# Late adaLN columns kept behind the low part of the weight unit ahead of them, in a two-layer decoder trunk on one core

## The chip, the cores and the metric

The kernel runs on one core of one Trainium2 chip. The metric is device time in microseconds of one launch, from the inputs in the chip's main memory to the output there; less is better. A core has TensorE for matmuls (PE in the profile, PEld for its weight loads), VectorE (DVE), ScalarE (ACT), GpSimd (POOL), SyncE (SP), which here only issues loads, and 16 DMA engines that all queues share.

## What is computed

The reference is a two-layer trunk with sequence 256 and width 1024 in f32. Cut to what matters here, one layer is:

```python
mod = c_act @ ada_w + ada_b                    # c_act = silu(c), one row; ada_w is 1024 x 3072
shift, scale, gate = jnp.split(mod, 3, axis=-1)
h = rmsnorm(x, norm_g) * (1.0 + scale[:, None]) + shift[:, None]
z = h @ w_in                                   # 1024 x 13312, feeds three branches and their gates
... # branch A: conv and linear recurrence; B: dilated attention; C: gated linear attention
merged = mg[:, :, 0] * (ya @ proj_a) + mg[:, :, 1] * (yb @ proj_b) + mg[:, :, 2] * (yc @ proj_c)
return x + gate[:, None] * (merged @ w_o)
```

`mod` is a matrix times one vector. Per layer it has 24 parts of 128 values, which the kernel calls columns: 0 to 15 are shift and scale (needed before the layer's first matmul), 16 to 23 the gate (needed when the layer ends).

## The kernel before

All weights are read once, as a stream. `layer_units()` lists the 144 units of a layer, `stream()` (L84) puts both layers' units and the columns into one list of items. A unit is 128 x 768 to 128 x 1024 f32; a column is the 128 x 1024 block of `ada_w` that one column of `mod` needs. In a layer the units come as: q, k, v and bg (0 to 15), branch A and attention projections (16 to 67), the gate mA (68 to 75), the projection pA (76 to 83), branch C in four heads, each of one cq, one ck and four c units (84 to 107), mC (108 to 115), pC (116 to 123), mB (124 to 131), pB (132 to 135) and wo (136 to 143).

Columns 0 to 15 of layer 0 stand among the first 16 units. The others stand later, one behind each third unit from unit 68 on (`REST`, L81): in layer 0 its own columns 16 to 23 and then columns 0 to 15 of layer 1, the last behind unit 137; in layer 1 its columns 16 to 23. That makes 24 columns in layer 0's second half and 8 in layer 1's, so that layer 1 has none from unit 90 on.

`load_next()` issues the DMA of the next item into one of six buffers named `raw`, on SP's queue, in the order of the list (L205 for units, L208 for columns). `advance(i)` prepares items up to unit i. For a unit, ScalarE rounds the weights to `whi` (L232), VectorE subtracts to get the low part `wlo` (L233), each in one of four buffers, so that a matmul in full f32 becomes three: hi by hi, hi by lo, lo by hi (L799 to L801 with the weights as the moving operand, L807 to L809 with them as the stationary one). For a column, `ada_tile()` multiplies the block with the activated conditioning vector and sums over the row in one VectorE instruction (L334, with a small one behind it that reads the accumulator); for a scale column one more small multiply follows (L336). The loop in `layer()` calls `advance(i + 3)` ahead of the matmuls of unit i. After an item is prepared, `load_next()` asks for the item six places on.

Beside the units' matmuls the branches run as generators that `pump()` moves on. In the part of a layer that matters here VectorE also does: rotary and scaling of q and k (L562 to L568 with GpSimd, L575), the attention's running minimum and reciprocal (L608, L611), the recurrence (L529 to L542), branch C's products (L666 to L689), and the merging of the branches (L915, L921, L922, L949 to L952).

The order of the instructions on each engine isn't that of the code. The kernel is built with a scheduler that models the engines' times and gives each engine its instructions in the order in which the model finds them ready. On the chip each engine then works through its list in that order and waits at the head of it. `tc.issue_after(x)` is a constraint on that scheduler: what is made within it comes behind the instruction x.

Of the kernel before, what the change touches and what calls it, by code (L numbers as in the profile page):

```python
# [10 lines left out]
F32 = mybir.dt.float32  # L11
# [3 lines left out]
ALU = mybir.AluOpType  # L15
# [57 lines left out]
def unit_elems(u):  # L73
    return {"T": 2 * u[4], "F": 1024, "P": 1024}[u[0]]
# [52 lines left out]
def hybrid_trunk(ctx: ExitStack, tc: tile.TileContext, ws, ada, vec, gates, a2, qkg, c_t, x_t, pos, inv, eye,  # L127
                 mask, tri, rst, out):
    nc = tc.nc
    V, A, G, T, SY = nc.vector, nc.scalar, nc.gpsimd, nc.tensor, nc.sync  # L130
# [53 lines left out]
    cur = {}  # L184


    raw_t, w_t = {}, {}
    at_item = [0, 0]
    early = {}

    def load_next():
        n = at_item[0]
        if n >= len(items):
            return
        at_item[0] += 1
        it = items[n]
        if it in early:
            raw_t[n] = early[it]
            cur["sy", "a", it[2]] = SY.dma_start(out=early[it], in_=ada[it[1], it[2]]).ins
            return load_next()  # L200
        if it[0] == "u":
            e = unit_elems(units[it[1]][1])
            o = offs[it[1]]
            t = wts.tile([P, e], F32, name="raw", tag="raw", bufs=NRAW)
            cur["sy", it[1]] = SY.dma_start(out=t, in_=ws[o:o + e * P].rearrange("(p n) -> p n", p=P)).ins  # L205
        else:
            t = wts.tile([P, D], F32, name="raw", tag="raw", bufs=NRAW)
            SY.dma_start(out=t, in_=ada[it[1], it[2]])  # L208
        raw_t[n] = t

    def advance(i):

        while at_item[1] < len(items):
            n = at_item[1]
            it = items[n]
            if it[0] == "u" and it[1] > i:
                return
            at_item[1] += 1
            r = raw_t.pop(n)
            if it[0] == "u":  # L220
                e = unit_elems(units[it[1]][1])


                streamed = units[it[1]][1][0] == "T" and units[it[1]][1][1] != "bg"
                o = 16 * ((it[1] % 2 == 0) != streamed)
                hi = wts.tile([P, D + 16], F32R, name="whi", tag="whi")[:, o:o + e]
                lo = wts.tile([P, D + 16], F32R, name="wlo", tag="wlo")[:, o:o + e]
                with ExitStack() as st:
                    if it[1] < 4:
                        st.enter_context(tc.issue_after(cur["ra"]))  # L230
                        st.enter_context(tc.issue_after(cur["rv"]))
                    A.copy(hi, r)  # L232
                    V.tensor_tensor(lo, r, hi.bitcast(F32), ALU.subtract)  # L233
                w_t[it[1]] = (hi, lo)
            else:
                ada_tile(it[1], it[2], r)
            load_next()


# [64 lines left out]
    def vcol(l, c, n=1):  # L304
        return vec_sb[:, l, c:c + n]
# [24 lines left out]
    def ada_tile(l, c, w):  # L330
        a, b = acc[:, l, c:c + 1], vec_sb[:, l, V_ADA + c:V_ADA + c + 1]
        j, i = (c // 2, c % 2) if c < 16 else (c - 16, 2)
        m = mod[:, l, i, j:j + 1]
        V.tensor_tensor_reduce(w, w, crow2, 1.0, b, ALU.mult, ALU.add, a if i == 0 else m)  # L334
        if i == 0:
            V.tensor_tensor(m, a, vcol(l, V_NG + j), ALU.mult)  # L336
        if l == 0 and i == 1:
            h_tile(0, j, cur["rstd"], cur["h"])
# [24 lines left out]
    def h_tile(l, j, rstd, h):  # L363
        hi, lo = h
        t = tmp()
        V.scalar_tensor_tensor(t, x_sb[:, j], mod[:, l, 0, j:j + 1], rstd, ALU.mult, ALU.mult)
        sh = mod[:, l, 1, j:j + 1]
        a = A.activation(hi[:, j], t, AF.Identity, bias=sh)  # L368
        v = V.scalar_tensor_tensor(lo[:, j], t, sh, hi[:, j].bitcast(F32), ALU.add, ALU.subtract)  # L369
        cur["h_last"] = (a.ins, v.ins)  # L370
# [443 lines left out]
    def layer(l, h, first_extra):  # L814
# [6 lines left out]
        for i in range(base, base + per_layer):  # L821
            kind, nm, p, kk, n = units[i][1]
            advance(4 * (i // 4) + 3 if i < 12 else i + LEAD)
            if i in first_extra:
                first_extra[i]()
# [255 lines left out]
```

## Time and profile before

| | us |
|---|---|
| three runs | 904.12, 908.38, 950.62; median 908.38 |
| the profiled execution | 906.63 |
| its span, first to last instruction | 904.9 |
| outside the span | 1.7 |

The profile is of one execution. Durations and waits come from it; a wait for several semaphores is put down to the one that came last. TensorE's matmuls are pipelined, and each is shown for about 0.28 us though one starts every 0.11 to 0.12 us. A gap between two starts is therefore shown as idle time only for the part that is longer than the matmul shown before it. Start times are microseconds from the start of the span.

### The profile page before, as it was taken

How to read it: one execution, taken by the hardware profiler on the slowest of the kernel's cores; microseconds unless marked ns; L12 is line 12 of the kernel's file. 1: busy time of each engine (PE TensorE's matmuls, PEld its weight loads, DVE VectorE, ACT ScalarE, POOL GpSimd, SP SyncE). 2: the span in 40 equal slices, each digit the busy share in tenths (PEclk: the TensorE clock that was granted, in tenths of full speed). 3: DMA queues.
4: the chain of work that ended last, by engine and by line, in shares of the span. 5: the costliest groups of instructions: out<-in, count | busy, mean ns of one | idle time of the engine just before them, and what ended most of it. 6: DMA issues, size and time to landing. Idle time of an engine off the chain costs nothing.

```text
span 904.9 us, 16407 instructions
## 1 busy us (share of the span) xinstructions
PE 865.6 (96%) x6340; PEld 818.7 (90%) x6340; DVE 671.9 (74%) x1115; ACT 531.8 (59%) x897; POOL 179.1 (20%) x160
## 2 busy tenths in 40 slices
PE   3989999999999999999999999989999999999998
PEld 2978999999988888998989999979999988899998
DVE  6998899669667667656776788986896666656674
ACT  4376976686544554644454689666874545554451
POOL 0026365224000110100030525651430001000000
PEclk7999999999999999999999999999999999999999
DMA  8884456446756666676654644553567455455651
GB/s 334 309 290 138 146 174 193 141 134 195 248 184 197 205 212 201 212 236 205 224 168 148 191 146 144 176 194 117 184 205 239 163 189 166 148 173 187 191 167 47
DMA packets 52111, 170.16 MB, mean 188 GB/s; under 512 B 6240, under 2 KB 8160, under 8 KB 52032
## 3 DMA queue, kind: packets, MB, share of 16 engines
q1 hardware_dynamic: 51216, 167.04, 56.8%
q10 hardware_dynamic: 672, 1.87, 0.7%
q8 instruction: 50, 0.82, 0.4%
q0 software_dynamic: 144, 0.20, 0.2%
q14 instruction: 29, 0.24, 0.1%
HBM read 168.23 MB, written 1.05 MB: 187 GB/s over the span
## 4 chain that ended last, share of the span: by engine, by line
PE 51%; DVE 19%; DMA 12%; issue 8%; ACT 5%; POOL 4%; DVEq 0%; SPq 0%; ACTq 0%
DMA raw<-in_ada_dram 10%; PE mm L807 10%; PE mm L809 10%; PE mm L808 10%; DVE wlo L233 8%; PE mm L799 5%; PE mm L800 5%; PE mm L801 4%; POOL ss L570 2%; PE xps L177 1%; ACT whi L232 1%; DVE raw L334 1%; DVE rb L564 1%; DMA g_raw<-in_gates_dram 1%; DVE ra L562 1%
## 5 line engine op out<-in xcount | busy, mean ns | idle before, releaser
L233 DVE TENSOR_TENSOR wlo<-raw,whi 128x1024 fp32r<-128x1024 f32 (+2 forms) x288 | 335.3, 1171 | 84.5 <-ACT whi L232 83.1
L232 ACT CAST whi<-raw 128x1024 fp32r<-128x1024 f32 (+2 forms) x288 | 280.1, 976 | 185.2 <-PE mm L808 120.4
L807 PE MATMUL mm<-hhi,whi 128*128 128x256 f32 x768 | 217.1, 283 | 2.9 <-DVE rb L564 2.9
L809 PE MATMUL mm<-hhi,wlo 128*128 128x256 f32 x768 | 216.0, 282 | 3.5 <-DVE wlo L233 3.5
L808 PE MATMUL mm<-hlo,whi 128*128 128x256 f32 x768 | 215.4, 280 | 0.0
L799 PE MATMUL mm<-whi,hhi 128*128 128x384 f32 (+2 forms) x480 | 169.5, 358 | 7.2 <-ACT hhi L368 6.5
L800 PE MATMUL mm<-wlo,hhi 128*128 128x384 f32 (+2 forms) x480 | 171.3, 358 | 1.6 <-DVE wlo L233 1.4
L801 PE MATMUL mm<-whi,hlo 128*128 128x384 f32 (+2 forms) x480 | 167.6, 355 | 0.5 <-DVE hlo L369 0.5
L807 PEld LDWEIGHTS mm<-hhi,whi 128*128 128x128 f32 x768 | 146.0, 190 | 4.5 <-ACT tmp L857 2.9
L809 PEld LDWEIGHTS mm<-hhi,wlo 128*128 128x128 f32 x768 | 145.6, 190 | 4.7 <-DVE wlo L233 4.1
L808 PEld LDWEIGHTS mm<-hlo,whi 128*128 128x128 f32 x768 | 145.7, 190 | 0.3
L799 PEld LDWEIGHTS mm<-whi,hhi 128*128 128x128 f32 x480 | 92.9, 195 | 14.5 <-ACT hhi L368 7.5
L800 PEld LDWEIGHTS mm<-wlo,hhi 128*128 128x128 f32 x480 | 93.4, 195 | 9.1 <-DVE wlo L233 3.2
L334 DVE CUSTOM_DVE_ANT_0 raw<-raw,crow,vec_sb 128x1024 f32<-128x1024 f32 x38 | 48.7, 1283 | 70.2 <-DMA raw<-in_ada_dram 70.2
L801 PEld LDWEIGHTS mm<-whi,hlo 128*128 128x128 f32 x480 | 92.5, 194 | 6.7 <-DVE hlo L369 0.8
L807 PE MATMUL mm<-yhi,whi 128*128 128x256 f32 x320 | 89.9, 281 | 1.5 <-DVE mg L949 1.5
L808 PE MATMUL mm<-ylo,whi 128*128 128x256 f32 x320 | 89.4, 279 | 0.0
L809 PE MATMUL mm<-yhi,wlo 128*128 128x256 f32 x320 | 89.2, 279 | 0.0
L807 PEld LDWEIGHTS mm<-yhi,whi 128*128 128x128 f32 x320 | 60.4, 189 | 2.5 <-DVE mg L949 1.7
L809 PEld LDWEIGHTS mm<-yhi,wlo 128*128 128x128 f32 x320 | 60.1, 188 | 0.8 <-DVE mod L334 0.4
L808 PEld LDWEIGHTS mm<-ylo,whi 128*128 128x128 f32 x320 | 60.1, 188 | 0.0
L708 POOL TENSOR_TENSOR at_hl<-att_sb,at_hl 128x384 fp32r<-128x384 f32 x8 | 8.8, 1096 | 206.3 <-ACT at_hl L707 206.3
(236 smaller groups left out, 1409.2 us busy)
## 6 DMA issues: line engine op xcount, KB each, us to landing
raw<-in_ws_dram SPq DMA_DIRECT2D x192, 512.0 KB, 4.2
raw<-in_ws_dram SPq DMA_DIRECT2D x88, 384.0 KB, 3.1
raw<-in_ada_dram SPq DMA_DIRECT2D x38, 512.0 KB, 4.5
raw<-in_ws_dram SPq DMA_DIRECT2D x8, 400.0 KB, 4.6
g_raw<-in_gates_dram ACTq DMA_DIRECT2D x3, 512.0 KB, 4.5
x_sb<-in_x_t_dram SPq DMA_DIRECT2D x2, 512.0 KB, 6.6
ada_yhi<-in_ada_dram SPq DMA_DIRECT2D x2, 512.0 KB, 7.8
ada_ylo<-in_ada_dram SPq DMA_DIRECT2D x2, 512.0 KB, 9.0
```

What stands on the lines that cost most here:

```text
L177: seen[0] = T.transpose(*a, **k).ins
L232: A.copy(hi, r)
L233: V.tensor_tensor(lo, r, hi.bitcast(F32), ALU.subtract)
L334: V.tensor_tensor_reduce(w, w, crow2, 1.0, b, ALU.mult, ALU.add, a if i == 0 else m)
L562: V.tensor_tensor(ra.rearrange("p (g s) d -> p g s d", g=3), z4, ctab[l][:, i, t].unsqueeze(2).to_broadcast(bc), ALU.mult)
L570: G.tensor_tensor(ss, ss, mhalf[:, 0:12].rearrange("p (a b) -> p a b", a=2), ALU.pow)
L799: T.matmul(o, ah, wh, start=(k == 0), stop=False)
L800: T.matmul(o, ah, wl, start=False, stop=False)
L801: T.matmul(o, al, wh, start=False, stop=(k == KT - 1))
L807: T.matmul(ps[:, 0:S], hi[:, a:b], xh[:, k], start=(k == 0), stop=False)
L808: T.matmul(ps[:, 0:S], hi[:, a:b], xl[:, k], start=False, stop=False)
L809: T.matmul(ps[:, 0:S], lo[:, a:b], xh[:, k], start=False, stop=(k == nk - 1))
```

## The change

A dictionary entry `cur["lo"]` now keeps the instruction that makes a unit's low part. A column that isn't one of the first 16 of layer 0 is made under the constraint that it comes behind the last such instruction, which is that of the unit just ahead of it in the stream. The first 16 are left as they were. Loads, buffers, arithmetic and the number of instructions stay.

```diff
     raw_t, w_t = {}, {}
+    early_cols = {(0, c) for c in range(16)}
...
                     A.copy(hi, r)
-                    V.tensor_tensor(lo, r, hi.bitcast(F32), ALU.subtract)
+                    cur["lo"] = V.tensor_tensor(lo, r, hi.bitcast(F32), ALU.subtract).ins
                 w_t[it[1]] = (hi, lo)
+            elif it[1:] in early_cols:
+                ada_tile(it[1], it[2], r)
             else:
-                ada_tile(it[1], it[2], r)
+
+                with tc.issue_after(cur["lo"]):
+                    ada_tile(it[1], it[2], r)
             load_next()
```

The lists of VectorE, ScalarE and TensorE change from layer 0's unit 68 on, and again in layer 1's. Lines of the changed kernel are one higher from L188 on and five higher from L242 on: L334 is L339 there, L233 is L234.

The first place is VectorE at layer 0's mB, where `ylo` (L642) makes branch B's low part. The number behind a name tells buffers' uses apart and grows along the stream: `raw_4316` to `raw_4416` are units, `raw_4320`, `raw_4419` and `raw_4522` are columns 12, 13 and 14 of layer 1. Before:

```order
L642 SCALAR_TENSOR_TENSOR ylo_4894<-sgb_767,yhi_4893 128x1024
L334 ISA raw_4419,mod_155<-raw_4419,crow_134,vec_sb_83 128x1024
L334 ISA mod_155 128x1
L233 TENSOR_TENSOR wlo_4720<-raw_4316,whi_4719 128x1024
L233 TENSOR_TENSOR wlo_4756<-raw_4352,whi_4755 128x1024
L233 TENSOR_TENSOR wlo_4788<-raw_4384,whi_4787 128x1024
L334 ISA raw_4522,acc_156<-raw_4522,crow_134,vec_sb_83 128x1024
```

After, at the same place:

```order
L647 SCALAR_TENSOR_TENSOR ylo_4894<-sgb_767,yhi_4893 128x1024
L234 TENSOR_TENSOR wlo_4720<-raw_4316,whi_4719 128x1024
L339 ISA raw_4320,acc_156<-raw_4320,crow_134,vec_sb_83 128x1024
L339 ISA acc_156 128x1
L341 TENSOR_TENSOR mod_155<-acc_156,vec_sb_83 128x1
L234 TENSOR_TENSOR wlo_4756<-raw_4352,whi_4755 128x1024
L234 TENSOR_TENSOR wlo_4788<-raw_4384,whi_4787 128x1024
L234 TENSOR_TENSOR wlo_4820<-raw_4416,whi_4819 128x1024
L339 ISA raw_4419,mod_155<-raw_4419,crow_134,vec_sb_83 128x1024
```

In the stream column 13 follows unit `raw_4416`. It stood three units ahead of that unit's low part; now it stands right behind it. Column 12 does the same with `raw_4316`.

The second place is VectorE in layer 0's pB, where the last column, `raw_4624`, ends up. The merging steps L949, L950 and L952 of pB are there; `raw_4588` is unit 136, `raw_4621` unit 137. After, with the column that stood ahead of all of these rows before:

```order
L234 TENSOR_TENSOR wlo_5002<-raw_4588,whi_5001 128x1024
L954 SCALAR_TENSOR_TENSOR mg_4717<-mg_4717,mm_5007 128x256
L957 SCALAR_TENSOR_TENSOR mlo_4966<-mrg_2938,mhi_4965 128x256 x2
L954 SCALAR_TENSOR_TENSOR mg_4717<-mg_4717,mm_5024 128x256
L955 TENSOR_TENSOR mrg_2938<-mrg_2938,mg_4717 128x256
L234 TENSOR_TENSOR wlo_5042<-raw_4621,whi_5041 128x1024
L955 TENSOR_TENSOR mrg_2938<-mrg_2938,mg_4717 128x256
L339 ISA raw_4624,mod_155<-raw_4624,crow_134,vec_sb_83 128x1024
```

The column has moved from ahead of pB's merging into the middle of it.

The third place is VectorE at the start of layer 0's mA. `wlo_2531` to `wlo_2570` are units 69 to 71, `raw_1936` and `raw_2099` the first two late columns, `ro_2458` the keys that TensorE transposes next, `ylo_188` branch A's low part. Before:

```order
L233 TENSOR_TENSOR wlo_2531<-raw_1971,whi_2530 128x1024
L233 TENSOR_TENSOR wlo_2549<-raw_2013,whi_2548 128x1024
L233 TENSOR_TENSOR wlo_2570<-raw_2059,whi_2569 128x1024
L608 ISA pr_2699,st_2692<-ps_s_2690,m1_sb_120 128x512
L608 ISA st_2692 128x1
L575 TENSOR_TENSOR ro_2458<-ro_2458,ss_2459 128x768
```

After:

```order
L339 ISA raw_1936,mod_155<-raw_1936,crow_134,vec_sb_83 128x1024
L339 ISA mod_155 128x1
L234 TENSOR_TENSOR wlo_2531<-raw_1971,whi_2530 128x1024
L547 SCALAR_TENSOR_TENSOR ylo_188<-rt_2184,yhi_187 128x1024
L234 TENSOR_TENSOR wlo_2549<-raw_2013,whi_2548 128x1024
L580 TENSOR_TENSOR ro_2458<-ro_2458,ss_2459 128x768
L234 TENSOR_TENSOR wlo_2570<-raw_2059,whi_2569 128x1024
```

Other work has moved with the columns: the scaling of the keys (L575, L580 after) has come ahead of a low part and of the attention's step (L608). On TensorE the transposes of these keys stand ahead of unit 70's first matmul after; before, they stood behind its tenth. Layer 1 shows the same pattern at its mA.

## Rows read from the trace of the kernel before

**Rows 1.** The page: busy time of each engine, share of span, instructions.

```profile
PE 865.6 (96%) x6340; PEld 818.7 (90%) x6340; DVE 671.9 (74%) x1115; ACT 531.8 (59%) x897; POOL 179.1 (20%) x160
```

**Rows 2.** VectorE's waits, first 200 to 450 us, then 676 to 722 us: total, times, longest.

```profile
DVE raw L334 <- DMA raw<-in_ada_dram: 60.7, 22, 4.7
...
DVE raw L334 <- DMA raw<-in_ada_dram: 8.9, 5, 2.6
```

**Rows 3.** TensorE's waits, 200 to 480 us, then 676 to 722 us: total, times, longest.

```profile
PE mm L809 <- DVE wlo L233: 2.2, 2, 1.8
PE mm L807 <- DVE mg L949: 1.5, 1, 1.5
PE xps L177 <- ACT pr L612: 1.3, 2, 1.0
...
PE xps L721 <- DVE g_hi L687: 0.9, 1, 0.9
PE xps L702 <- DVE ke L678: 0.5, 1, 0.5
PE xps L720 <- ACT cv L686: 0.3, 1, 0.3
...
PE xps L177 <- ACT pr L612: 0.8, 1, 0.8
```

**Rows 4.** Busy time by stretch: stretch, width, PE, PEld, DVE, ACT, POOL, clock, DMA share, GB/s.

```profile
229.00:282.00 53.00, 51.45 (x446) 48.79 (x446) 35.35 (x62) 28.78 (x48) 0.00 (x0) 1.00 0.62 204
673.00:725.00 52.00, 51.20 (x447) 48.86 (x447) 35.22 (x61) 29.00 (x49) 0.00 (x0) 1.00 0.62 205
283.00:433.00 150.00, 145.98 (x1052) 134.18 (x1051) 101.90 (x177) 73.28 (x125) 9.59 (x13) 0.99 0.66 212
726.00:868.00 142.00, 142.00 (x1051) 131.71 (x1050) 86.40 (x131) 73.09 (x123) 8.26 (x12) 1.00 0.55 176
433.00:454.00 21.00, 19.37 (x163) 18.82 (x162) 16.22 (x32) 9.70 (x15) 0.00 (x0) 1.00 0.67 215
868.00:887.00 19.00, 19.00 (x165) 19.00 (x164) 14.01 (x29) 8.35 (x14) 0.00 (x0) 1.00 0.36 115
```

**Rows 5.** VectorE's timeline at layer 0's mB: start, us, what, idle before.

```profile
418.01 1.28 DVE L334 CUSTOM_DVE_ANT_0 raw<-raw,crow,vec_sb 128x1024 f32<-128x1024 f32 x1 [2.76 <-DMA raw<-in_ada_dram]
419.22 0.08 DVE L334 DVE_READ_ACCUMULATOR2_ANT mod<- 128x1 f32 x1
419.22 3.49 DVE L233 TENSOR_TENSOR wlo<-raw,whi 128x1024 fp32r<-128x1024 f32 x3
```

**Rows 6.** TensorE's timeline behind that, then the stretch around it.

```profile
418.38 0.28 PE L808 MATMUL mm<-hlo,whi 128*128 128x256 f32 x1
420.50 0.52 PE L809 MATMUL mm<-hhi,wlo 128*128 128x256 f32 x1 [1.83 <-DVE wlo L233]
...
418.00:426.00 8.00, 6.17 (x40) 5.96 (x39) 4.70 (x5) 2.54 (x4) 0.00 (x0) 0.79 0.67 206
```

**Rows 7.** VectorE's timeline at layer 0's pB.

```profile
436.24 1.28 DVE L334 CUSTOM_DVE_ANT_0 raw<-raw,crow,vec_sb 128x1024 f32<-128x1024 f32 x1 [4.67 <-DMA raw<-in_ada_dram]
...
437.45 2.35 DVE L233 TENSOR_TENSOR wlo<-raw,whi 128x1024 fp32r<-128x1024 f32 x2
439.72 0.74 DVE L949 SCALAR_TENSOR_TENSOR mg<-mg,mm 128x256 f32<-128x256 f32 x2
```

**Rows 8.** The page, DMA issues: what, queue, count, KB each, median us to landing.

```profile
raw<-in_ws_dram SPq DMA_DIRECT2D x192, 512.0 KB, 4.2
raw<-in_ada_dram SPq DMA_DIRECT2D x38, 512.0 KB, 4.5
```

**Rows 9.** VectorE, GpSimd and TensorE timelines at layer 0's mA.

```profile
225.46 0.95 DVE L575 TENSOR_TENSOR ro<-ro,ss 128x768 f32<-128x768 f32 x1
...
221.65 3.13 POOL L570 TENSOR_TENSOR ss<-ss,mhalf 128x12 f32<-128x12 f32 x1
...
227.22 0.82 PE L177 MATMUL xps<-eye_sb,ro 128*128 128x128 f32 x6
```

## The prediction

> **What bounds the kernel now.** The page's busy times come first: TensorE is busy 865.6 of 904.9 us, VectorE 671.9 [rows 1]. So TensorE's own work sets most of the time, and only what makes it stand still, or lowers its clock, can be won here. Second, VectorE's waits in the two stretches that hold the late columns [rows 2]: it stood 60.7 us in 22 waits and 8.9 us in 5 for columns' loads, 69.6 us in all. That isn't yet time lost. Third, therefore, TensorE's own waits in the same stretches [rows 3]: 2.2 us for low parts, 1.5 for pB's merging, 1.3 and 0.8 for the attention's probabilities, 0.9, 0.5 and 0.3 in branch C, 7.5 in all. Of ten microseconds that VectorE waits, about one reaches TensorE.
>
> The fourth view gives the size better, because the kernel has a copy of itself without late columns: layer 1 from unit 90 on. Rows 4 pair the stretches. From branch C to the end of mB layer 0 takes 150.0 us (283 to 433) and layer 1 takes 142.0 (726 to 868), with 1052 and 1051 matmuls; the layer with columns shows 4.0 us of TensorE idle, the other none. At pB and the start of wo it is 21.0 (163 matmuls) against 19.0 (165). At mA and pA both layers have columns, and idle is 53.00 - 51.45 = 1.55 and 52.00 - 51.20 = 0.80 us.
>
> The fifth view is one case from close by. At 418.01 a column begins after VectorE waited 2.76 us for its load; then three low parts follow without a pause [rows 5]. 2.76 + 1.28 + 0.08 + 3.49 is 7.6 us in which their turn was late. TensorE needs a low part and stands until 420.50, 1.83 us; and the granted clock of 418 to 426 is 0.79, that is, after standing the engine ran for a time at the lower of its two levels, 1.2 instead of 2.4 GHz [rows 6]. The 8 us gave (1 - 0.79) x 8 = 1.7 us less work than the full clock, on top of the 1.83.
>
> **Why the order did that.** VectorE works through its list in order. Before, a column stood three units ahead of its place in the stream, so its load was the youngest one wanted; a load takes 4.5 us from issue to landing [rows 8]. A unit's 24 matmuls at about 0.115 us are 2.8 us. A low part is made three units early, 8.3 us, of which cast and subtraction take about 2.3; a delay of up to about 6 us is hidden. Most waits (60.7 / 22 = 2.8 us, and 1.36 for the column itself) fit in that, which is why only a few reach TensorE.
>
> **The change part by part.** It adds and removes no instruction and no load. It moves 32 columns of 1.28 + 0.08 us on VectorE [rows 5], and with them the scheduler moves other work on VectorE, ScalarE and TensorE. SP's queue keeps its order. A column now comes six items after its load was asked for, and at least four units lie between, 4 x 2.8 = 11 us against 4.5 to land. So I take the 69.6 us of waiting as gone. Nothing is late next in its place on VectorE: in the long stretch it was busy 101.9 of 150 us [rows 4]. What TensorE gets back:
>
> 1. Branch C to mB of layer 0. At most 150.0 - 142.0 = 8.0 us: 4.0 idle, 1.7 clock, and 2.3 of gaps too short to show, since a matmul is drawn longer than its turn. At least 0, if other work is late instead. I take 7.0, near the top, because layer 1's stretch is the same program and the only thing it lacks is the columns; 1.0 is left for the columns' own time, which stays.
> 2. pB and wo of layer 0. At most 21.0 - 19.0 = 2.0. Before, the last column waited 4.67 us, and pB's first merging step came only at 439.72 [rows 7], for which TensorE stood 1.5 us [rows 3]. Now the column stands in the middle of pB's merging, with 1.36 us. If all of that is on the path and nothing else is won, the end is 1.4 us later. Between -1.4 and 2.0 I take 1.0: the 1.5 us go, and part of the column comes back.
> 3. mA and pA of both layers. At most their idle, 1.55 + 0.80 = 2.35; at least below nothing, because here the order of other work changes too (third place of the change, and the second rival). I take 1.0.
>
> The sum is 7.0 + 1.0 + 1.0 = 9.0 us. The profiled execution took 906.63, so 897.6 is forecast. That execution is 1.75 below the median of the runs shown (908.38) and 2.5 above their lowest.
>
> The Trainium skill has a page, "Perfetto Trace Analysis", whose section "Identifying Performance Opportunities" says that improving a kernel means, in general, improving its most-contended engine. By that rule a new order on VectorE would bring nothing here, and the sum would be 0. The trace doesn't bear that out in full: 8.0 us lie between two stretches with the same matmuls. But the first rival below is that case. The same page says under "Optimization Strategy" that a gap which repeats can mean too few buffers. By that, the six load buffers would be at fault, no order of VectorE would help, and the third rival would hold; 11 us of lead against 4.5 us of landing speak against it.
>
> **The rivals.** First, the waits are hidden anyway, and TensorE's gaps only move. For it: TensorE is 96% busy, nine tenths of VectorE's waiting never reached it, and the new order of TensorE's list comes from a model that may again put small transposes too early, as it did where 1.3 and 0.8 us were lost for probabilities. Against it: layer 1's stretch, which a list of the same origin serves with no idle time. With the gaps of [rows 3] replaced by as many new ones and the clock's 1.7 us won, it gives 904.9; with two thirds replaced, 906.6 - 1.7 - 2.5 = 902.4. I call 902 to 907 this case.
>
> Second, slower: the keys' transposes at mA. Before, VectorE scaled the keys at 225.46, GpSimd's factor was there at 221.65 + 3.13 = 224.8, and TensorE took the transposes at 227.22 [rows 9]. After, TensorE comes to them ten matmuls earlier, 227.22 - 1.15 = 226.1, while on VectorE a column (1.36) and branch A's low part (1.2) have come ahead of the scaling and one attention step (0.8) has gone behind it. With one column less earlier on, it would end at about 226, with no slack. If it comes d late, TensorE stands for d, and where it stands long the lower clock costs another 1.7, as in [rows 6]. The pattern is in both layers: 2 x (d + 1.7). It eats the 9.0 us from d = 2.8 on; with d = 4 it is 906.6 - 9.0 + 11.4 = 909.0. For it speaks that GpSimd's part varies and nothing waits behind it before; against it, that at most two VectorE instructions can be that late.
>
> Third, the change doesn't do what it says: columns still wait for their loads behind the low parts, because a buffer comes free later. The loads are then what the path hangs on, and the gaps stay, about 906. Against it stands the lead of 11 us.
>
> **How the numbers follow.** The forecast, 893.5 to 902 with 897.6 as its middle, gets 0.66; the first rival 0.20; the slower one 0.07; the third 0.04; more than the bounds allow (12.35 us, 894.3, less an execution's luck) 0.03. The range reaches from 893.5 over most of the first rival and the third to 906.0, and leaves out about 0.15. A measurement of this kernel can tell about 2% from no change, that is 18 us. The bounds of the terms stop at 12.35 us, so faster by over 2% gets only 0.03; slower by over 2% would need several times the second rival, 0.01; within 2% the rest, 0.96.
>
> **What would show each step right or wrong.** In the changed kernel's list of VectorE's waits the row of columns waiting for their loads should fall from 69.6 us to under 8. Layer 0's stretch from branch C to mB should have almost no TensorE idle and last 142 to 144 us, at a granted clock of 1.00; pB to wo should last 19 to 21. TensorE's waits for low parts, L721 and L702 should be gone there. The keys' transposes at mA should show no wait over 1 us in either layer. The prediction is wrong if the stretch stays over 147 us, if columns still wait for loads, or if TensorE's new list shows waits over 1.5 us with a lowered clock behind them.

## The result and the profile after

| | before | after |
|---|---|---|
| median of four runs each, us | 906.69 | 892.39 (891.68 to 894.17) |
| ratio after to before | | 0.9848, 95% interval 0.9824 to 0.9873 |
| the profiled execution, us | 906.63 | 892.15 |
| its span, us | 904.9 | 890.3 |

The change takes 1.5% off, 14.3 us by the medians and 14.5 by the profiled executions. It is less than the 2% that a measurement was taken to tell from no change, but the interval is clear of 1. One of the four runs before took 950.62 us, a slow one that the ratio leaves out; the median of the other three is 905.01, and against that the difference is 12.6 us. The forecast was 897.6, the range ended at 893.5, and the median lies 1.1 us below that.

The page of the changed kernel, busy times, the line that answers to [rows 1]:

```profile
PE 860.3 (97%) x6340; PEld 816.5 (92%) x6340; DVE 677.8 (76%) x1115; ACT 533.0 (60%) x897; POOL 176.7 (20%) x160
```

VectorE is busy 5.9 us longer than before, and the kernel is 14 us shorter. Nothing became cheaper. What went is waiting. The page's chain of waits, shares by engine, first of the kernel before:

```profile
PE 51%; DVE 19%; DMA 12%; issue 8%; ACT 5%; POOL 4%; DVEq 0%; SPq 0%; ACTq 0%
```

and of the changed kernel:

```profile
PE 71%; DVE 13%; issue 5%; POOL 4%; ACT 4%; DMA 1%; SPq 0%; DVEq 0%; ACTq 0%
```

12% of the span hung on transfers, now 1%. The page's costliest groups, the columns of the changed kernel (busy time, mean ns of one, idle time ahead of them):

```profile
L339 DVE CUSTOM_DVE_ANT_0 raw<-raw,crow,vec_sb 128x1024 f32<-128x1024 f32 x38 | 50.3, 1325 | 0.0
```

The last number is 0.0: VectorE waits for no column's load any more, where it stood 69.6 us in the two stretches of [rows 2]. TensorE's waits from 200 to 480 us, the view of [rows 3], have two lines left, both of the layer's end and as long in the kernel before (1.0 and 0.9 us), and from 640 to 720 us there is none:

```profile
PE mm L159 <- DVE rs_m L356: 1.0, 1, 1.0
PE xps L945 <- ACT tmp L379: 0.9, 1, 0.9
```

The stretches of [rows 4] in the changed kernel. The cuts lie at the same distance from the first matmul of a stage (mA, branch C, pB, wo) as there, so that nearly the same matmuls are in each: mA and pA of layer 0, of layer 1, branch C to mB of layer 0, pB and the start of wo of layer 0.

```profile
228.43:279.32 50.89, 50.89 (x446) 48.66 (x445) 36.57 (x64) 29.82 (x49) 0.00 (x0) 1.00 0.65 227
659.32:710.26 50.94, 50.94 (x447) 48.70 (x446) 36.63 (x64) 29.84 (x49) 0.00 (x0) 1.00 0.67 225
280.32:422.08 141.76, 141.76 (x1052) 131.64 (x1051) 106.76 (x177) 73.95 (x125) 9.64 (x13) 1.00 0.70 227
422.08:441.36 19.28, 19.28 (x167) 19.28 (x166) 16.01 (x34) 9.72 (x15) 0.00 (x0) 1.00 0.66 211
```

Against [rows 4] these are 2.11 us (53.00 - 50.89), 1.06 (52.00 - 50.94), 8.24 (150.00 - 141.76) and 1.72 (21.00 - 19.28) shorter, with 446, 447, 1052 and 167 matmuls where there were 446, 447, 1052 and 163. The last pair isn't like for like: by matmuls, from pB's third to the 163rd behind it, it is 433.10 to 454.39 before and 422.18 to 441.25 after, 21.29 against 19.07 and so 2.2 us shorter. In all four TensorE is busy over the whole width. Layer 0 with its columns now takes what layer 1 took without them (142.0, 19.0). With 2.2 for the last the four add up to 13.6 us; 1.0 more of the 14.6 us in the span lies outside of them.

What a column's place means is read at column 13, the one of [rows 5]. SyncE's queue and VectorE in the changed kernel, the issue of its load and its turn:

```profile
402.28 0.33 SPq L209 DMA_DIRECT2D raw<-in_ada_dram  x1
```

```profile
413.37 1.28 DVE L339 CUSTOM_DVE_ANT_0 raw<-raw,crow,vec_sb 128x1024 f32<-128x1024 f32 x1
```

That is a lead of 11.1 us. In the kernel before, the same load was issued here,

```profile
412.22 0.33 SPq L208 DMA_DIRECT2D raw<-in_ada_dram  x1
```

and VectorE came to it at 418.01 - 2.76 = 415.25 [rows 5]: a lead of 3.0 us, for a load that took 5.8 to land.

### The profile page after: what moved, and what is told of

Its sections match the earlier page's. It is cut to its first block, busy times and chain, and to the rows that moved or that the text cites. A ratio compares the mean times of both kernels' runs of the same rounds, so it can differ in the third digit from the quotient of the medians.

```text
span 890.3 us, 16392 instructions
## 1 busy us (share of the span) xinstructions
PE 860.3 (97%) x6340; PEld 816.5 (92%) x6340; DVE 677.8 (76%) x1115; ACT 533.0 (60%) x897; POOL 176.7 (20%) x160
## 4 chain that ended last, share of the span: by engine, by line
PE 71%; DVE 13%; issue 5%; POOL 4%; ACT 4%; DMA 1%; SPq 0%; DVEq 0%; ACTq 0%
PE mm L812 14%; PE mm L814 14%; PE mm L813 14%; PE mm L806 6%; PE mm L805 6%; PE mm L804 6%; DVE wlo L234 4%; POOL ss L575 2%; PE xps L177 2%; PE xps L173 2%; PE ps_s L173 1%; DVE rb L569 1%; DVE ra L567 1%; POOL ro L573 1%; ACT whi L233 1%
## 5 line engine op out<-in xcount | busy, mean ns | idle before, releaser
L234 DVE TENSOR_TENSOR wlo<-raw,whi 128x1024 fp32r<-128x1024 f32 (+2 forms) x288 | 336.5, 1172 | 109.4 <-ACT whi L233 107.6
L233 ACT CAST whi<-raw 128x1024 fp32r<-128x1024 f32 (+2 forms) x288 | 280.3, 977 | 206.8 <-PE mm L813 126.3
L339 DVE CUSTOM_DVE_ANT_0 raw<-raw,crow,vec_sb 128x1024 f32<-128x1024 f32 x38 | 50.3, 1325 | 0.0
```

Source lines behind the costliest of these rows:

```text
L234: cur["lo"] = V.tensor_tensor(lo, r, hi.bitcast(F32), ALU.subtract).ins
```

## The experiments

Each was timed beside the kernel before on the same chip, whose medians in the four sessions were 906.5 to 908.9 us. Stretches are those of the last table, cut in the same way.

| run | what | median us (range) | ratio to before, 95% interval |
|---|---|---|---|
| c1_after_again | the changed kernel again | 892.52 (892.29 to 894.74) | 0.9849 [0.9824, 0.9873] |
| e1_no_cols | columns' arithmetic left out | 893.28 (891.47 to 893.86) | 0.9838 [0.9795, 0.9882] |
| e3_first_layer | order in layer 0's half only | 894.16 (893.69 to 895.57) | 0.9854 [0.9811, 0.9897] |
| e4_second_layer | order in layer 1's half only | 905.20 (902.65 to 906.49) | 0.9964 [0.9943, 0.9984] |
| e5_one_free | column 13 set free | 892.61 (891.63 to 893.66) | 0.9831 [0.9780, 0.9883] |
| e8_back1 | one unit earlier | 891.66 (890.54 to 892.26) | 0.9823 [0.9787, 0.9859] |
| e8_back2 | two units earlier | 893.02 (892.68 to 894.22) | 0.9842 [0.9812, 0.9872] |
| e8_back3 | three units earlier | 893.42 (892.64 to 895.65) | 0.9848 [0.9816, 0.9880] |
| e8_back4 | four units earlier | 902.33 (899.29 to 906.91) | 0.9942 [0.9921, 0.9962] |
| e7_five_buffers | five load buffers | 893.76 (892.42 to 895.00) | 0.9846 [0.9822, 0.9869] |
| e10_five_back3 | five buffers, three units earlier | 910.43 (907.77 to 913.57) | 1.0026 [1.0009, 1.0044] |
| e9_triple | columns three times | 900.37 (898.40 to 900.77) | 0.9916 [0.9885, 0.9947] |
| e11_one_wait | one wait, at mB | 892.24 (891.54 to 894.87) | 0.9839 [0.9816, 0.9863] |
| e12_wait_pB | one wait, ahead of pB | 894.47 (893.73 to 895.09) | 0.9864 [0.9842, 0.9886] |
| e13_wait_pA | one wait, at pA | 892.59 (892.09 to 893.56) | 0.9845 [0.9819, 0.9871] |

### Do the columns' own 1.3 us cost anything?

```diff
                 with tc.issue_after(cur["lo"]):
-                    ada_tile(it[1], it[2], r)
+                    V.tensor_copy(mod[:, it[1], i, j:j + 1], r[:, 0:1])
```

> The changed kernel with the 32 late columns' reduction on VectorE (1.3 us each) replaced by a copy of one element of the loaded block, at the same place; the columns' products are left out, their loads stay. Theory (the gain came from taking away VectorE's waits for the columns' loads; the columns' own 1.3 us lie beside TensorE's work): 891.4 to 893.4 us, within 1 us of the changed kernel's 892.4, and the stretches of TensorE (branch C to mB of layer 0, pB, wo) as long as in the changed kernel to 0.5 us. Rival (VectorE's amount of work still bounds the stages with columns): the 24 late columns of layer 0 and the 8 of layer 1 are worth 32 x 1.3 = 42 us of VectorE, and if a tenth of it lay on the path the time is 888 us or less.

It was 893.28, no faster than with the columns. Its stretches from branch C to mB and at pB:

```profile
281.23:423.28 142.05, 142.05 (x1052) 131.75 (x1051) 89.13 (x155) 73.81 (x125) 9.75 (x13) 1.00 0.69 227
423.28:442.56 19.28, 19.28 (x167) 19.28 (x166) 14.10 (x31) 9.70 (x16) 0.00 (x0) 1.00 0.64 210
```

VectorE is busy 89.13 us there in place of 106.76, and TensorE takes 142.05 in place of 141.76. At mA and pA alone it is 0.5 us less a layer (50.35 and 50.40), which the whole time doesn't show. So from branch C to pB a column in its place is free, in the middle of pB's merging too.

### Which half of the stream gives the gain?

```diff
-            elif it[1:] in early_cols:
+            elif it[1:] in early_cols or n > 200:
```

> The changed kernel with the order kept only for the 24 late columns that stand in layer 0's half of the stream; the 8 of layer 1 stand free, as before. Theory (each stage pays for the waits of its own columns): layer 0's terms stay (mA and pA 2.1, branch C to mB 8.2, pB and wo 2.1, start 0.5), layer 1's 1.2 at pA and 0.4 ahead of it come back: 893.5 to 894.5 us. Rival (the gain is one thing, the half-speed stretch of the clock after 420 us and where the later ones fall): 891.5 to 893 us, as the changed kernel.

`n` is the item's number in the stream. It was 894.16, as the theory had it. Layer 0's stretches are the changed kernel's to 0.01 us, and the stretch of mA and pA in layer 1 is back at 52.44. The other half has `n < 200` there:

> The other half: the order kept only for the 8 late columns of layer 1; the 24 of layer 0 stand free. Theory: layer 0's stages as in the kernel before, pA of layer 1 at 29.2 us in place of 30.4: 904.5 to 906 us, 1.2 to 2 us under the kernel before, and with the kernel of layer 0's half the two gains add up to 14.3 within 1 us. Rival (the two halves are worth little apart, since the columns of one half push the other's loads about): the two gains add up to 12 us or less.

905.20; the stretch in layer 1 is 50.95, as in the changed kernel. But the two gains, 908.93 - 894.16 = 14.8 and 908.93 - 905.20 = 3.7, add up to 18.5, where the theory had 14.3 within 1 and the rival 12 or less. The whole gain on this chip is known only from a neighbour of the changed kernel, the run with column 13 set free: 908.93 - 892.61 = 16.3. And the interval of this run leaves anything from 1.5 to 5.2 us for the smaller gain. So the excess of about 2 us isn't clear of the noise. One source of that noise stands in layer 0 of this run, whose instructions come in the very order of the kernel before on VectorE, ScalarE and TensorE. Its stretches there, in an execution of 902.65 us, the fastest of ten:

```profile
228.81:280.96 52.15, 51.72 (x446) 49.20 (x446) 35.33 (x63) 28.78 (x48) 0.00 (x0) 1.00 0.67 208
...
281.96:428.97 147.01, 143.73 (x1052) 132.50 (x1051) 101.76 (x177) 73.45 (x125) 9.34 (x13) 1.00 0.69 215
428.97:452.33 23.36, 21.04 (x167) 20.84 (x166) 16.31 (x33) 9.87 (x16) 0.00 (x0) 0.93 0.62 201
```

The same order gave 53.00, 150.00 and 21.00 in [rows 4]: 1 to 3 us more or less in a stage, between two executions. The stretches of the changed kernel, which has no such waits, came out the same to the hundredth in its second profile (50.89, 50.94, 141.76 and 19.28). So an execution of the kernel before is one draw among several, its stretches too; 13 of them on that chip lay between 903.98 and 911.79.

### Place or lead: how far ahead may a column stand?

A list `los` of all units' low parts lets a column be held behind an earlier one:

```diff
-                with tc.issue_after(cur["lo"]):
+                with tc.issue_after(los[-2]):
```

(`los[-3]`, `los[-4]` and `los[-5]` for two, three and four units.)

> The changed kernel with each late column held behind the low part of one unit earlier in the stream. Theory (what a column loses is its load's lead: behind its own unit it has four to five units, 11 to 14 us, against 4.5 us to land; one unit less leaves 8 to 11 us): no waits for columns' loads, 892 to 893.5 us. Rival (what counts is that the column stands ahead of the low part that is due next, whether or not it waits): a third of the gain goes back, 896 to 898 us.

> The same with two units earlier. Theory: the lead is 5.5 to 8 us, so a few columns wait, 10 us of waits or less in all, and 892.5 to 897 us. Rival: two thirds of the gain go back, 901 to 903 us.

> The same with three units earlier, which is about where the columns stood in the kernel before. Theory: the lead is 2.8 to 5.5 us, most columns wait, 40 to 70 us in all, and the time is 900 to 908 us with a stand of TensorE of over 1 us in mB or pB of layer 0. Rival (the gain came from the other work that moved on the engines when the columns were put under a constraint at all): below 897 us.

With one and two units there is no wait for a column's load and the time is 891.66 and 893.02. With three it is still 893.42, far from the 900 to 908 that the theory gave. VectorE's waits for columns there, in total, times and longest:

```profile
DVE raw L341 <- DMA raw<-in_ada_dram: 5.0, 7, 1.3
```

The theory had the place of the columns before wrong by one: most of them stood ahead of four low parts that come before them in the stream, not three (in VectorE's list of the kernel before, 4 for most, 3 to 5 for the rest). So four was run.

> Each late column held behind the low part of four units earlier, so that four low parts that come before it in the stream are still to be made when it is worked on, as in the kernel before; with three to be made it was 893.4 us. Theory (the step is sharp, because with six buffers a column's load can't be asked for until the item six places ahead is done, and with four low parts still to come that item is the one just ahead of it on VectorE; with three there is one unit's time between): waits for columns' loads of 50 to 70 us in all, and 900 to 907 us. Rival (the constraint moved other work too, and that gave the gain): 892 to 896 us.

902.33, and the waits are back:

```profile
DVE raw L341 <- DMA raw<-in_ada_dram: 52.2, 26, 4.4
```

One unit of difference is worth 8.9 us, and the constraint as such isn't what gave the gain. But 5.9 us (908.20 - 902.33) of the gain stay even here. In this order no column stands ahead of five low parts, where 6 of the 32 did before; what else goes into the 5.9 wasn't tested.

Why the step is so sharp: a load is issued when VectorE has set a buffer free. At column 13 with four units that is the end of a low part at 406.20 + 1.22 = 407.42. One more unit's low part and branch B's lie between it and the column's turn at 413.20 - 2.71 = 410.49. That is a lead of 3.0 us, as in the kernel before, for a load that lands after 5.8:

```profile
407.45 0.33 SPq L210 DMA_DIRECT2D raw<-in_ada_dram  x1
```

```profile
413.20 1.28 DVE L341 CUSTOM_DVE_ANT_0 raw<-raw,crow,vec_sb 128x1024 f32<-128x1024 f32 x1 [2.71 <-DMA raw<-in_ada_dram]
```

With three units, two units' low parts and branch B's lie between, and the lead is 5.06 us, just enough. (The expectation had none between with four and one with three; VectorE's list has one more in both.)

```profile
400.97 0.33 SPq L210 DMA_DIRECT2D raw<-in_ada_dram  x1
```

```profile
406.03 1.28 DVE L341 CUSTOM_DVE_ANT_0 raw<-raw,crow,vec_sb 128x1024 f32<-128x1024 f32 x1
```

To tell the place from the lead, the place of three units was kept and a buffer taken away.

```diff
-    NRAW = 6
+    NRAW = 5
```

> The changed kernel with five load buffers in place of six; the columns stay behind their own unit. Theory: a load is asked for one item later, which leaves a column three to four units, 8 to 11 us, against 4.5 us to land: no waits of over 1 us for columns, 891.5 to 895 us. Rival (six buffers were just enough for the units' own loads): ScalarE waits for units' loads, and 897 us or more.

> Five load buffers, and each late column held behind the low part of three units earlier: the place that gave 893.4 us with six buffers, but with the load asked for one item later, right ahead of the column. Theory (what counts is the time between the asking for a load and the column's turn, not the place): waits of 30 to 70 us for columns' loads and 898 to 908 us, above the kernel with five buffers and the columns behind their own unit by 5 us or more. Rival (what counts is the place): no more than 1.5 us above that kernel.

Five buffers alone cost about 1.3 us by the medians (893.76 against 892.4 to 892.5), which the spread of the runs doesn't tell from nothing; there is no wait of VectorE for a column, and the stretches of the second half are the changed kernel's to 0.01 us. Five buffers with the columns three units earlier took 910.43, 16.7 us more, above the theory's 908 and more than the kernel before. Same place for 28 of the 32 columns (4 stand one unit later), one buffer's lead less, and the waits are there. At column 13 the lead is 2.2 us (419.09 - 2.17 - 414.68):

```profile
414.68 0.33 SPq L210 DMA_DIRECT2D raw<-in_ada_dram  x1
```

```profile
419.09 1.28 DVE L341 CUSTOM_DVE_ANT_0 raw<-raw,crow,vec_sb 128x1024 f32<-128x1024 f32 x1 [2.17 <-DMA raw<-in_ada_dram]
```

VectorE's waits for columns in this run, then TensorE's waits from 200 to 480 us:

```profile
DVE raw L341 <- DMA raw<-in_ada_dram: 44.0, 24, 4.4
```

```profile
PE mm L814 <- DVE mg L956: 3.6, 1, 3.6
PE xps L177 <- ACT pr L619: 2.5, 1, 2.5
```

So the lead decides, not the place. But it has fewer waits than the kernel before (44.0 us in 24 against 70.2 in 28) and loses more: the total of VectorE's waits isn't the price either. Its waits stand where they hurt, ahead of pB's merging and, in both layers, ahead of the attention's step that the probabilities hang on: the stretches of mA and pA are 55.46 and 55.71 us, pB and wo 24.67, but branch C to mB only 142.37.

### Does a hold of VectorE cost the same wherever it is?

```diff
                     ada_tile(it[1], it[2], r)
+                    for _ in range(2):
+                        V.tensor_tensor_reduce(r, r, crow2, 1.0, vec_sb[:, 0, 0:1], ALU.mult, ALU.add, spare)
```

> The changed kernel with each late column's reduction done three times, so that VectorE is held 2.6 us longer at each of the 32 columns, 83 us in all, about the length of the waits of the kernel before (2.6 us each), but at the new place, where no load is waited for; the repeats change the columns' values, and with them the result. Theory (a hold of VectorE costs TensorE only by the place at which it stands; a hold of about 4 us behind the column's own unit fits in the 6 us that a low part is early): within 2 us of the changed kernel, 891.5 to 894.5 us. Rival (the total of VectorE's lost time made the loss, wherever it stood): 83 against 69.6 us lost before, so the whole 14.3 us come back, 906 to 910 us.

900.37, 8 us above the changed kernel: neither the theory's 2 nor the rival's 14. The scheduler knew of the repeats and put other work between them. The profiled execution took 898.40, 6 us above the changed kernel's. TensorE's waits from 200 to 480 us show where most of it went:

```profile
PE mm L816 <- DVE mlo L960: 2.8, 2, 1.8
...
PE mm L815 <- DVE mg L957: 0.9, 1, 0.9
```

The stretch of pB and wo's start is as wide as before, 19.28 us, but TensorE is busy 15.56 of it, with 128 matmuls in place of 167: wo's first matmuls wait for the merged sums that VectorE makes late. 3.7 of the 6 us are these waits; the rest wasn't taken apart. So VectorE's time isn't free everywhere either; around pB it is on the path, once there is 2.6 us more of it at each column.

### What does one wait cost?

First a column was set free, in the hope that it would go back to its old place.

```diff
-            elif it[1:] in early_cols:
+            elif it[1:] in early_cols or it[1:] == (1, 13):
```

> The changed kernel with one column set free again, the one that VectorE waited for at 418 us before (column 13 of layer 1's set, ahead of mB). Theory (the single wait there cost TensorE its 1.83 us stand and then 1.7 us at half the clock): if it is put back at the same place in VectorE's row, mB of layer 0 is 3 to 4.4 us longer than its 22.1, the granted clock falls near 420 us again, and the time is 895 to 897 us. Rival (the stand needed several waits one after the other, the loads being late only in a crowd): mB within 1 us of 22.1 and 892 to 893.4 us.

892.61, but the scheduler put it ahead of three low parts, not four, and its wait was 0.5 us; this run tells nothing of a wait of 3 us. So the column was made when the item six places ahead had been prepared, and the next low parts were put behind it (shown for the run at mB, the other two differ in the column's number; it is skipped at its later place):

```diff
             load_next()
+            if n == nf - NRAW:
+                ahead.add(nf)
+                with tc.issue_after(cur["lo"]):
+                    cur["col"] = ada_tile(1, 13, raw_t[nf])
...
                     A.copy(hi, r)
+                    if n > nf - NRAW and ahead:
+                        st.enter_context(tc.issue_after(cur["col"]))
```

> The changed kernel with one single column (13 of layer 1's set, at mB of layer 0) worked on as early as its load's buffer allows and held there, ahead of four low parts, as in the kernel before; the other 31 stay behind their own unit. VectorE should wait 2.5 to 4.5 us for its load. Theory (one wait of about 3 us and the column's 1.4 fit in the 6 us that a low part is early; it is the waits one after another that use this up): mB of layer 0 within 0.7 us of 22.1, and 892 to 893.5 us. Rival (the single wait at 418 us was the cause of the 4.4 us at mB): mB 25.5 to 26.5 us, the granted clock falls behind it, and 895.5 to 897 us.

VectorE's timeline of this run, the column's turn at mB, and the stretch from branch C to mB:

```profile
407.13 1.29 DVE L349 CUSTOM_DVE_ANT_0 raw<-raw,crow,vec_sb 128x1024 f32<-128x1024 f32 x1 [3.19 <-DMA raw<-in_ada_dram]
```

```profile
280.88:422.64 141.76, 141.76 (x1052) 131.69 (x1051) 106.38 (x177) 73.94 (x125) 9.64 (x13) 1.00 0.72 228
```

A wait of 3.19 us, longer than the 2.76 of [rows 5], ahead of the same low parts, and the stretch is 141.76 to the hundredth. Alone, it costs nothing. In the kernel before it stood in a row of waits, 22 in that half [rows 2]; that these had used up the time that low parts are early is argued. What fits it: in four runs VectorE's waits for columns from branch C to mB come to 20.6, 30.5, 42.6 and 45.0 us (five buffers and three units; four units; layer 1's half alone; the kernel before), and the stretch is 0.6, 3.2, 5.3 and 8.2 us longer than 141.76. But the columns' places differ among these too, and no run changed the row alone.

> The changed kernel with one single column (15 of layer 1's set, the last) worked on as early as its load's buffer allows, ahead of four low parts and of pB's merging in layer 0; the other 31 stay behind their own unit. VectorE should wait about 4.5 us. Theory (a wait costs by what stands behind it on VectorE; here it is the merging that has to empty the accumulators for pB's next matmuls, which has little slack): pB of layer 0 0.7 to 1.7 us longer than its 11.3, TensorE waits for the merging again, and the time is 0.7 to 1.7 us above the changed kernel's. Rival (one wait is hidden wherever it is): pB within 0.3 us of 11.3.

The column waited 5.31 us, and pB's stretch is 1.66 us longer, with 161 matmuls in place of 167:

```profile
422.66:443.60 20.94, 18.87 (x161) 18.47 (x160) 17.41 (x35) 9.95 (x15) 0.00 (x0) 1.00 0.60 193
```

```profile
PE mm L823 <- DVE mg L965: 2.1, 2, 1.6
```

The six matmuls at about 0.115 us are 0.7 us more, so like for like it is 2.3 us, above the theory's 0.7 to 1.7 and all that the change won at pB (2.2). The whole time is 1.95 us above the changed kernel's on the same chip. This wait is also the longest of the three single ones; that its place counts is read from TensorE's list, which names the merging and no low part.

> The same with column 20 of layer 0's own set, which is worked on ahead of the attention's last step in layer 0 then (the running minimum that the probabilities and their transposes hang on). VectorE should wait 3 to 4.5 us. Theory: pA of layer 0 1 to 2.2 us longer than its 29.2, TensorE waits for the probabilities, and the time is as much above the changed kernel's. Rival (one wait is hidden wherever it is): pA within 0.3 us of 29.2.

Here VectorE waited 2.31 us, less than expected, the attention's step stood one low part behind the column, and the stretch is 51.14 in place of 50.89: 0.25 us, the rival's side. In the kernel before, the wait was 3.19 us and the attention's step stood right behind it:

```profile
244.03 1.28 DVE L334 CUSTOM_DVE_ANT_0 raw<-raw,crow,vec_sb 128x1024 f32<-128x1024 f32 x1 [3.19 <-DMA raw<-in_ada_dram]
...
245.24 0.69 DVE L608 CUSTOM_DVE_ANT_0 pr<-ps_s,m_sb 128x512 f32<-128x512 f32 x1
```

So at pA one wait of 2.3 us is hidden. That the longer one cost what [rows 4] showed there is argued from the five-buffer run, where a wait of that kind (3.76 us) went with TensorE's 2.5 us for the probabilities; it was not isolated.

## Why the prediction was wrong, and where it was right

The mechanism was right; the sizes of all three terms were too small. The columns' waits are gone whole, as were the waits on the low parts, L721 and L702; the lead of column 13 is the 11 us that were worked out; branch C to mB takes 141.76 us at a granted clock of 1.00 without idle time, where 142 to 144 were named; pB to wo 19.28, where 19 to 21 were. What failed are the sizes that were taken inside the bounds, and the bounds themselves, of which each was passed.

- Term 1, branch C to mB, bounds 0 to 8.0, taken 7.0, measured 8.24. The 1.0 was "left for the columns' own time, which stays". The run without the columns' arithmetic shows that this time costs nothing (142.05 against 141.76): layer 1's stretch was the full measure.
- Term 2, pB and wo, bounds -1.4 to 2.0, taken 1.0, measured 1.72 by the cut and 2.2 by matmuls. The upper bound set 163 matmuls before against 165 in layer 1; two more at 0.115 us make it 2.2, so it was itself a little low. And "part of the column comes back" was wrong for the same reason as in term 1: 19.28 with the column in the middle of the merging, 19.28 without it. The single wait put back there costs 2.3 like for like, so the term is about the size of this one wait.
- Term 3, mA and pA, at most 1.55 + 0.80 = 2.35, taken 1.0, measured 2.11 + 1.06 = 3.17. This bound was itself too low. It took shown idle time for the whole gap, though a matmul is drawn longer than its turn, which the working of term 1 says in its own words. The discount on top was for the second rival, and that one fell: the keys' transposes have no wait in either layer.
- Outside the terms 1.0 us, for which the sum had nothing: 0.6 ahead of layer 0's mA, the rest between wo and layer 1's mA. The changed kernel's second profile came to mA of layer 0 at 218.80 us, its first at 218.37, the kernel before at 218.94, so part of this is the difference between two executions; how much isn't settled.

So the sum's three discounts took 3.35 us off bounds of 12.35, and the range's low end trusted that the bounds "stop at 12.35 us", where the three terms gave 13.6. Term 1 charged 1 us for the columns' own time, although VectorE was busy only 101.9 of 150 us there [rows 4]; with that cover the run without the columns found nothing to charge.

One more step was off without entering the sum. "A column stood three units ahead of its place in the stream": it was four for most, and that one unit is more than half of the effect (893.4 against 902.3).

The first rival (gaps only move) fell: no new gap came. The second fell as said. The third, that the loads are late wherever the columns stand, fell too. Of the rule that was weighed there, from the Trainium skill's page "Perfetto Trace Analysis", section "Identifying Performance Opportunities", that one improves a kernel, in general, by improving its most-contended engine, the prediction drew a gain of 0. That reading was too narrow, by 14.3 us: an engine busy 74% was put in another order, and TensorE, whose work stayed, stopped waiting for it. The same page of the Trainium skill has it under "Optimization Strategy" that a repeating gap can mean too few buffers. The trace agrees in one order and not in the other: with the columns three units early, six buffers against five are worth 17 us; with the columns in their place, about 1.3 us, which isn't clear of the noise.

## What to carry to other kernels

On an engine that works through its list in order, put work that nobody waits for behind the work that somebody does, and far enough behind the issue of its own load: here a lead of 5 us was enough, 3 us was not, and one unit of place was worth 9 us. Price a wait by what stands behind it, not by its length alone: of three single waits 3.2 us cost nothing, 2.3 cost 0.25 and 5.3, ahead of the merging, cost 2.3. Compare two stretches at equal numbers of matmuls. Where the same program has a stretch without the suspected cost, take the difference whole, and discount it only for something that a row shows.

## What the hardware showed that was not expected

Whether the granted clock falls after a stand of TensorE isn't told by the stand's length. In [rows 6] a stand of 1.83 us was followed by the lower level. A stand of 2.32 us ahead of pB (the run with layer 1's half alone) was so too, but one of 2.05 us at the same place (columns four units earlier) was not. The stretches behind these two, in that order:

```profile
437.00:441.00 4.00, 4.00 (x25) 4.00 (x26) 4.00 (x10) 1.94 (x4) 0.00 (x0) 0.68 0.88 312
```

```profile
435.00:439.00 4.00, 3.72 (x31) 3.72 (x32) 4.00 (x11) 1.69 (x3) 0.00 (x0) 1.00 0.88 314
```

25 matmuls in 4 us at a granted clock of 0.68, against 31 in 3.72 us at 1.00. Which stands bring the lower clock with them stays open. Where one does, it costs what TensorE loses behind it too, and that may be a part of the spread between executions of the kernel before; the changed kernel has no such stand at mB or pB.
